# Output projection as seven block products, late modulation sums on ScalarE with adding transfers

## The chip, the cores and the metric

The kernel runs on one core of a Trainium2 chip. The metric is the device time of one execution in microseconds. The engines are TensorE (PE; its weight loads are listed as PEld), VectorE (DVE), ScalarE (ACT), GpSimd (POOL) and SyncE (SP). SP and POOL issue the transfers; transfers that add to what is in memory (`accum_op`) are issued by POOL.

## The reference, cut

One residual block on x (512 tokens x 1024) with a conditioning vector c. Everything is float32.

```python
mod = silu(c) @ w_ada + b_ada      # shift1, scale1, gate1, shift2, scale2, gate2
h = rms_norm(x, g_pre_mix) * (1 + scale1) + shift1
z = h @ w_in                       # [GLU | q latent | kv latent | rotary key | gates]
u = ua * sigmoid(ub)
u = silu(layer_norm(causal_depthwise_conv(u, 31 taps)))
y_a = u @ w_conv_out
y_b = mla_attention(...) @ w_attn_out          # 8 heads
y = (sigmoid(g_a) * y_a + sigmoid(g_b) * y_b) @ w_out
x = x + gate1 * rms_norm(y, g_post_mix)
h = rms_norm(x, g_pre_mlp) * (1 + scale2) + shift2
x = x + gate2 * rms_norm(relu(h @ w_mlp_in)**2 @ w_mlp_out, g_post_mlp)
```

## The kernel before, in words

**Number format.** A float32 product is made of three fp32r products (`mm3`, L476): each operand is split into a high part (a ScalarE cast) and a low part (a VectorE difference). `split` (L481) does that for an operand, `W` (L494) for a loaded weight, and `wunit` (L514) loads and splits one. So each 1024-wide weight costs one cast and one difference.

**Order of the work.** The code does not issue instructions at once. Every call is recorded as an `Op` (`Planner.record`, L262), and all of them are issued by one line, L410, which is why every row of the profile names L410. `Planner.plan` (L325) gives each operation a due time, worked back from TensorE's sequence with a price for each operation (`cost`, L234), and then runs a list schedule in which each engine takes the ready operation of the earliest due time, less its `hurry` (L346); TensorE takes the ready one of the lowest rank, which is its order in the program less a `boost`. `plan.after` adds a dependence on an earlier operation. The result is one fixed order for each engine; engines and transfer queues work in that order. Buffers come from two arenas in on-chip memory, `f_arena` (22400 words a partition) and `r_arena` (28000, for the split parts), and from eight PSUM banks. `Arena.alloc` (L90) places buffers with the lifetimes of the pass before, up to 14 passes are made, and the plan that is shortest by the planner's own prices is issued.

**Stages.** First the modulation for the first norm and the input projection; then the latents and the attention, head by head (`proj`, `scores`, `pv`). VectorE fills its time with the 31-tap convolution: `pump(n)` (L836) puts n of its 248 taps at a place in the program. Then come the attention's output product, the two gate products, the layer norm, and the conformer's product with `co_evac` (L1324), which forms the mixed tensor (gate a times y_a plus gate b times y_b) and splits it.

**Late modulation.** Parts 2, 3 and 4 of the modulation (gate1, shift2, scale2) are needed only after the output projection. `ada_units` (L1167) loads w_ada in units of 256 rows x 1024 columns (1 MB), twelve units in all, and sums them on VectorE, eight operations of 1024 columns for each part. `take` (L1184) puts units at places in the program, here from the gate products on. `late_mod` (L1359) adds the partitions up with TensorE and forms the gate row `G1` and the columns `mod[:, 2]` and `mod[:, 3]`.

**Output projection.** 192 fp32r products of 512 columns: token tile by token tile (four of 128), two halves of 512 output columns, eight blocks of 128 input rows, three products each. All tiles' first halves are made first (`ys[t, 0]`), then the late modulation, then the second halves, tile by tile. After two tiles (`for tp in range(2)`, L1411) these are normed (squares on ScalarE, the power on POOL, the scaling and the residual sum on VectorE), normed again for the MLP, written out, transposed on TensorE and scaled and split into `h2`, the MLP's input. The first hidden products of the MLP work on 256 columns (the first two token tiles), so that they can run while the other two tiles are finished.

**MLP.** The second MLP product is already made by `strassen` (L1486) in four chunks: seven products of 256 x 512 blocks with sums and differences of blocks for eight products. Each of its products needs up to one left operand (a 1024-wide sum and a split) and one right operand (two 1024-wide weights, their difference and splits). Partial results are added to memory (`y_spill`) with adding transfers of 256 KB on POOL.

Of the kernel before, what the change touches and what calls it, by code (L numbers as in the profile page):

```python
# [51 lines left out]
ADAS = (1, 1, 0, 4)  # L52
KGRP = ((2,), (3,), (4,), (5,), (6,), (7,))
# [361 lines left out]
def tile_hybrid_block(  # L415
# [30 lines left out]
    hD = [tc.dram_tile([P, KD * T], F32, name=f"h_spill{i}") for i in range(2)]  # L446
    yD = [tc.dram_tile([P, D], F32, name=f"y_spill{t}") for t in range(NT)]
# [16 lines left out]
    def emit(past, replay):  # L464
# [682 lines left out]
        rope_half(0)  # L1147
        proj(0)
        proj(1)
        scores(0)  # L1150
        for h in range(H):
            if h + 2 < H:
                proj(h + 2)
            if h == 2:
                rope_half(1)
            if h + 1 < H:
                scores(h + 1)
            pv(h)
            pump(PUMPS[2])
        for q in qkv:  # L1160
            ra.free(*q)
        ra.free(K1, K2)


# [151 lines left out]
        take(late, ADAS[3])  # L1316
# [5 lines left out]
        mT = []  # L1322

        def co_evac(ct, b):  # L1324
            m = fa.alloc(T)
            dve.scalar_tensor_tensor(fa.v(m), fa.v(ta[ct]), 1.0, pb.v(b), op0=ALU.add, op1=ALU.mult)
            dve.tensor_tensor(fa.v(m), fa.v(m), fa.v(yb[ct]), ALU.add)
            hl = pair(T)
            split(fa.v(m), *hl)
            mT.append(hl)  # L1330
            fa.free(m, ta[ct], yb[ct])
            take(late, ADAS[0])

# [25 lines left out]
        def late_mod():  # L1359
            G1 = gate_row(2, g_post_mix, 0.5)  # L1360
# [18 lines left out]
        xr = []  # L1379
        for t in range(NT):  # L1380
            b = fa.alloc(D)
            sp.dma_start(out=fa.v(b), in_=x[t * P:(t + 1) * P, :])
            xr.append(b)
        h2, h2f, h2s_ = [], [], {}

        def k4(a):
            return a.rearrange("p (k t) -> p k t", k=4)

        def yl(t, k):
            return ra.v(mT[k][0])[:, t * P:(t + 1) * P], ra.v(mT[k][1])[:, t * P:(t + 1) * P]  # L1390

        ys = {(t, 0): pb.alloc() for t in range(NT)}
        for k0 in range(0, KD, 2):
            w = wunit(w_out, k0, 0, 2, 512)
            for k in range(2):
                for t in range(NT):
                    mm3(pb.v(ys[t, 0]), yl(t, k0 + k), w(k, 0, 512), k0 + k == 0, k0 + k == KD - 1)
            w.free()
        take(late)
        G1 = late_mod()  # L1400
        ys.update({(t, 1): pb.alloc() for t in range(NT)})
        wo = [wunit(w_out, k0, 512, 2, 512) for k0 in range(0, KD, 2)]
        NCH = 4
        HPC = FF // P // NCH

        def hid_weights(n0, n, i0=0):

            return {(i, kh): wunit(w_mlp_in, 4 * kh, (n0 + i) * P, 4, 256) for i in range(i0, n, 2) for kh in range(2)}

        ws0 = {(0, 0): wunit(w_mlp_in, 0, 0, 4, 256)}  # L1410
        for tp in range(2):  # L1411
            xn = []
            for t in (2 * tp, 2 * tp + 1):
                for k in range(KD):
                    mm3(pb.v(ys[t, 1]), yl(t, k), wo[k // 2](k % 2, 0, 512), k == 0, k == KD - 1)
                    if t == NT - 1 and k % 2 == 1:
                        wo[k // 2].free()
# [383 lines left out]
```

## Time and profile before

| | |
|---|---|
| median of 3 runs | 813.99 us (813.33 to 814.12) |
| the profiled execution | 812.54 us, span 810.4 us |
| granted TensorE clock | 0.998 |
| TensorE busy | 790.7 us |
| VectorE busy | 738.0 us |
| ScalarE busy | 472.0 us |
| POOL busy | 62.8 us |
| bytes moved | 131.00 MB |

Busy time counts the union of an engine's instructions; matmuls are pipelined, so the mean duration in a row is longer than the time that each takes of the engine. A row of a group gives line, engine, operation, tile written and tiles read, shapes and count, then busy us and mean ns of one, then the idle time of the engine before them and who ended it. All tiles in the two arenas carry the arena's name. "CUSTOM_DVE_ANT_0" is the VectorE instruction that also sums (`tensor_tensor_reduce`).

### The profile page before, as it was taken

What the parts mean: (1) busy time and instruction counts of PE and PEld (TensorE: products, weight loads), DVE (VectorE), ACT (ScalarE), POOL (GpSimd) and SP (SyncE); (2) the same over time, 40 slices, a digit from 0 to 9 for tenths busy, and PEclk for the clock granted to TensorE, in tenths of its full rate; (3) what the DMA queues carried; (4) which work ended last, traced back from release to release, by engine and by line L of the source; (5) the groups of instructions that cost most, each with busy time, mean ns of one, the idle gap of its engine ahead of it and who ended that gap; (6) DMA issues with size and microseconds to landing.
All of it is one profiled execution on the core that took longest, in us unless ns stands there. A gap on an engine that the chain in (4) does not pass through costs nothing. (4 is left out here: it accounts for less than half of the span.)

```text
span 810.4 us, 11974 instructions
## 1 busy us (share of the span) xinstructions
PE 790.7 (98%) x4450; PEld 687.7 (85%) x4450; DVE 738.0 (91%) x1045; ACT 472.0 (58%) x784; POOL 62.8 (8%) x121
## 2 busy tenths in 40 slices
PE   6999999999999999999999999999999999999996
PEld 3778988889897888888888879988998899889985
DVE  3898999999999999999997579899689999996997
ACT  5455463365885247229243378677667756777851
POOL 2001010000000000000000021001002200320023
PEclk9999999999999999999999999999999999999999
DMA  9989433112352160064998044159317991895076
GB/s 295 313 247 341 144 116 110 53 53 66 105 170 78 53 202 5 1 222 162 344 391 281 7 159 148 53 149 266 132 53 157 243 343 37 171 288 178 28 164 134
DMA packets 99981, 131.00 MB, mean 162 GB/s; under 512 B 8433, under 2 KB 67154, under 8 KB 99922
## 3 DMA queue, kind: packets, MB, share of 16 engines
q1 hardware_dynamic: 93586, 118.69, 45.1%
q0 software_dynamic: 6336, 11.54, 8.9%
q8 instruction: 35, 0.57, 0.3%
q14 instruction: 24, 0.20, 0.1%
HBM read 109.23 MB, written 20.97 MB: 161 GB/s over the span
## 5 line engine op out<-in xcount | busy, mean ns | idle before, releaser
L410 PE MATMUL psum<-r_arena 128*128 128x512 f32 (+3 forms) x4108 | 751.1, 344 | 4.0 <-DVE f_arena L410 1.6
L410 PEld LDWEIGHTS psum<-r_arena 128*128 128x128 f32 x4108 | 647.6, 189 | 91.7 <-ACT r_arena L410 2.7
L410 ACT CAST r_arena<-f_arena 128x1024 fp32r<-128x1024 f32 (+5 forms) x249 | 235.2, 966 | 137.3 <-PE psum L410 86.4
L410 DVE TENSOR_TENSOR r_arena<-f_arena,r_arena 128x1024 fp32r<-128x1024 f32 (+5 forms) x259 | 276.1, 1093 | 28.0 <-PE psum L410 15.1
L410 DVE SCALAR_TENSOR_TENSOR f_arena<-f_arena,cw 128x512 f32<-128x512 f32 x240 | 164.2, 737 | 0.0
L410 DVE TENSOR_TENSOR f_arena<-f_arena 128x1024 f32<-128x1024 f32 (+3 forms) x108 | 113.6, 1071 | 4.7 <-ACT f_arena L410 2.4
L410 ACT ACTIVATE f_arena<-f_arena 128x512 f32<-128x512 f32 (+4 forms) x121 | 71.3, 607 | 42.9 <-DVE f_arena L410 42.0
L410 ACT COPY f_arena<-psum 128x512 f32<-128x512 f32 (+4 forms) x103 | 55.3, 547 | 41.5 <-PE psum L410 36.9
L410 DVE SCALAR_TENSOR_TENSOR f_arena<-f_arena,cT 128x256 f32<-128x256 f32 (+1 forms) x70 | 55.9, 800 | 1.2
L410 POOL DMA_DIRECT2D y_spill<-f_arena x40 | 34.8, 879 | 263.6 <-ACT f_arena L410 254.8
L410 ACT ACTIVATE f_arena<-psum 128x512 f32<-128x512 f32 x43 | 25.2, 593 | 45.4 <-PE psum L410 44.3
L410 PE MATMUL psum<-ident,f_arena 128*128 128x128 f32 (+1 forms) x234 | 34.8, 288 | 7.9 <-DVE f_arena L410 7.9
L410 PEld LDWEIGHTS psum<-ident,f_arena 128*128 128x128 f32 (+1 forms) x234 | 28.3, 147 | 14.0 <-DVE f_arena L410 9.3
L410 ACT CAST r_arena<-psum 128x512 fp32r<-128x512 f32 (+2 forms) x57 | 30.0, 562 | 12.7 <-PE psum L410 12.4
L410 DVE TENSOR_TENSOR r_arena<-psum,r_arena 128x512 fp32r<-128x512 f32 (+2 forms) x57 | 35.6, 653 | 0.9 <-ACT r_arena L410 0.6
L410 DVE TENSOR_TENSOR f_arena<-psum,f_arena 128x512 f32<-128x512 f32 (+1 forms) x34 | 22.3, 666 | 7.7 <-PE psum L410 7.6
L410 POOL TENSOR_TENSOR stats<-stats,nhalf 128x1 f32<-128x1 f32 (+1 forms) x17 | 15.5, 915 | 172.3 <-ACT stats L410 156.3
L410 POOL TENSOR_TENSOR lns<-lns,nhalf 128x4 f32<-128x4 f32 x1 | 1.4, 1400 | 249.5 <-DVE lns L410 249.5
L410 ACT ACTIVATE r_arena<-f_arena 128x256 fp32r<-128x256 f32 (+3 forms) x17 | 10.9, 642 | 14.4 <-DVE f_arena L410 11.3
L410 ACT ACTIVATE r_arena<-f_arena,mod 128x512 fp32r<-128x512 f32 x8 | 6.5, 816 | 21.6 <-DVE mod L410 21.6
L410 DVE TENSOR_SCALAR f_arena<-f_arena,stats 128x1024 f32<-128x1024 f32 x8 | 6.0, 753 | 13.6 <-POOL stats L410 13.6
L410 DVE CUSTOM_DVE_ANT_0 f_arena<-psum,mask 128x128 f32<-128x128 f32 (+3 forms) x32 | 14.6, 481 | 0.0
(98 smaller groups left out, 211.1 us busy)
## 6 DMA issues: line engine op xcount, KB each, us to landing
f_arena<-in_w_ada_dram SPq DMA_DIRECT2D x16, 1024.0 KB
f_arena<-in_w_mlp_in_dram SPq DMA_DIRECT2D x32, 512.0 KB
f_arena<-in_w_mlp_out_dram SPq DMA_DIRECT2D x32, 512.0 KB
f_arena<-in_w_in_dram SPq DMA_DIRECT2D x24, 512.0 KB
y_spill<-f_arena POOLq DMA_DIRECT2D x40, 256.0 KB, 6.2
f_arena<-in_w_ada_dram SPq DMA_DIRECT2D x32, 256.0 KB
f_arena<-in_x_dram SPq DMA_DIRECT2D x8, 512.0 KB
h_spill<-r_arena SPq DMA_DIRECT2D x16, 256.0 KB
```

What stands on the lines that cost most here:

```text
L410: getattr(self.real[o.eng], o.fn)(*o.a, **o.k)
```

## The change

It has three parts. First, the output projection is made by `strassen`, which gets a function for its left operand and a function `used` that is called when the first half of it is no longer needed. The mixed tensor is kept as two float32 buffers `mF` (not split). `mix_block` receives each block of results: the first contribution to a block is copied from PSUM, the second is added to it, and a tile that is complete is normed, and a pair of complete tiles goes through `to_hidden` (the second half of the old loop). `late_mod` is called once the first block is complete, after the second of seven products. Second, the late sums are made in the attention: each unit is loaded, multiplied by its column of silu(c) on ScalarE in place, and written (the first of a part, SP) or added (the other seven, POOL) to a buffer `aD` in memory; `late_mod` loads the three sums. Third, in `strassen` itself the difference s3, the split of block 22 and the difference t3 are recorded ahead of the fifth product.

```diff
+ADAQ = (1, 1, 1, 2, 2, 2, 2, 1)
+ADAH = 5e4
...
+    aD = {q: tc.dram_tile([P, D], F32, name=f"a_spill{q}") for q in (2, 3, 4)}
...
+        def ada_sums(parts):
+            for part in parts:
+                for u in range(4):
+                    plan.hurry, plan.after = ADAH, len(plan.ops) - 1
+                    b = fa.alloc(2 * D)
+                    v = fa.v(b, "p (j n) -> p j n", j=2)
+                    sp.dma_start(out=v, in_=w_ada[u * 256:(u + 1) * 256, part * D:(part + 1) * D].rearrange("(j p) n -> p j n", p=P))
+                    plan.after = None
+                    for jj in range(2):
+                        j = u * 2 + jj
+                        act.mul(v[:, jj], v[:, jj], cT[:, j:j + 1])
+                        if j == 0:
+                            sp.dma_start(out=aD[part], in_=v[:, jj])
+                        else:
+                            pool.dma_start(out=aD[part], in_=v[:, jj], accum_op=ALU.add)
+                    fa.free(b)
+                    plan.hurry = 0.0
+                    yield
...
+        late = ada_sums((2, 3, 4))
         for h in range(H):
...
             pv(h)
             pump(PUMPS[2])
+            take(late, ADAQ[h])
...
-        late = ada_units((2, 3, 4))
-            if ct % 2:
-                take(late, ADAS[2])
-        take(late, ADAS[3])
...
         def co_evac(ct, b):
-            m = fa.alloc(T)
-            dve.scalar_tensor_tensor(fa.v(m), fa.v(ta[ct]), 1.0, pb.v(b), op0=ALU.add, op1=ALU.mult)
-            dve.tensor_tensor(fa.v(m), fa.v(m), fa.v(yb[ct]), ALU.add)
-            hl = pair(T)
-            split(fa.v(m), *hl)
-            mT.append(hl)
-            take(late, ADAS[0])
+            if ct % 4 == 0:
+                mF.append(fa.alloc(4 * T))
+            m = k4(fa.v(mF[-1]))[:, ct % 4]
+            dve.scalar_tensor_tensor(m, fa.v(ta[ct]), 1.0, pb.v(b), op0=ALU.add, op1=ALU.mult)
+            dve.tensor_tensor(m, m, fa.v(yb[ct]), ALU.add)
...
         def late_mod():
+            for part in (2, 3, 4):
+                ada_acc[part] = load(D, aD[part])
...
-        def strassen(hv, block, banked, parts=1):
+        def strassen(A, block, banked, used, parts=1):
...
             dve.tensor_tensor(a3(s4), A(0, 1), a3(s2), ALU.subtract)
-            product(a_form(a3(s4)), b_form(b22), bb, False)
+            s3 = fa.alloc(1024)
+            dve.tensor_tensor(a3(s3), A(0, 0), A(1, 0), ALU.subtract)
+            used()
+            w22 = b_form(b22)
+            t3 = b12
+            b_sub(t3, b22, b12)
+            fa.free(*b22)
+            product(a_form(a3(s4)), w22, bb, False)
...
+        def mix_block(mi, nh, bs):
+            n = seen[mi, nh] = seen.get((mi, nh), 0) + 1
+            done = n == (1 if (mi, nh) == (1, 0) else 2)
+            for tt in range(2):
+                t = 2 * mi + tt
+                y, ps, s = fa.v(ysb[t])[:, sl], pb.v(bs[tt]), nrm[t]
+                if not done:
+                    act.copy(y, ps)
+                    continue
+                if (mi, nh) == (1, 0):
+                    y = ps
+                else:
+                    dve.tensor_tensor(y, ps, y, ALU.add)
...
+                        dve.tensor_tensor_reduce(ra.v(j), y, y, 0.25 / D, s[:, 1:2], ALU.mult, ALU.add, s[:, 2:3])
+                    pool.tensor_tensor(s[:, 2:3], s[:, 2:3], nhalf[:, :1], ALU.pow)
...
+                xr = load(D, x[t * P:(t + 1) * P, :])
...
+            if xn:
+                to_hidden(mi, xn)
+            if (mi, nh, n) == (0, 0, 2):
+                G1[0] = late_mod()
...
+        strassen(lambda i, j: k4(fa.v(mF[j]))[:, :, 256 * i:256 * i + 256], blocks_of(w_out, 0), mix_block,
+                 lambda: fa.free(mF[0]))
```

The rest of `mix_block` and `to_hidden` are the steps of the old loop over `tp`, moved.

More of the change, by code (lines that the diff above doesn't have):

```diff
@@ L1145, in pv @@
                     ra.free(vh, vl)
[L1147 to L1162, printed above, removed]
         ada_acc = {}
@@ L1187, in take @@
                     return
-        late = ada_units((2, 3, 4))
+        late = ada_sums((2, 3, 4))
+        rope_half(0)
+        proj(0)
+        proj(1)
+        scores(0)
+        for h in range(H):
+            if h + 2 < H:
+                proj(h + 2)
+            if h == 2:
+                rope_half(1)
+            if h + 1 < H:
+                scores(h + 1)
+            pv(h)
+            pump(PUMPS[2])
+            take(late, ADAQ[h])
+        for q in qkv:
+            ra.free(*q)
+        ra.free(K1, K2)
         def feat_gemm(wsrc, c0, rhs, evac, pumped=0, groups=(2, 2, 2, 2)):
@@ L1467, in emit @@
-        fa.free(G1)
-        def h2s(k, a, n):
-            return tuple(ra.v(b)[:, a:a + n] for b in h2[k])
-        ysb = {}
-        G2, fin = None, []
-        late = ada_units((5,))
+        h2, h2f, h2s_ = [], [], {}
         def blocks_of(wsrc, k0):
@@ L1556, in strassen @@
             pb.free(*bb)
-            s3 = fa.alloc(1024)
-            dve.tensor_tensor(a3(s3), A(0, 0), A(1, 0), ALU.subtract)
-            t3 = b12
-            b_sub(t3, b22, b12)
             product(a_form(a3(s3)), b_form(t3), ba, False)
-            fa.free(s3, *t3, *b22)
+            fa.free(s3, *t3)
             banked(1, 1, ba)
@@ new lines, in to_hidden @@
+        def to_hidden(tp, xn):
+            if tp == 1:
+                fa.free(mF[1])
+                ws0[0, 1] = wunit(w_mlp_in, 4, 0, 4, 256)
+                ws0.update(hid_weights(0, 4, 2))
+            if tp == 0:
+                ws0[0, 0] = wunit(w_mlp_in, 0, 0, 4, 256)
+                h2[:] = [pair(T) for _ in range(KD)]
+                h2f[:] = [fa.alloc(4 * T) for _ in range(2)]
+            hsl = slice(tp * 256, (tp + 1) * 256)
+            for k2 in range(KD // 2):
+                b = pb.alloc()
+                for q in range(2):
+                    for t in range(2):
+                        k = 2 * k2 + q
+                        pe.transpose(pb.v(b)[:, (2 * q + t) * P:(2 * q + t + 1) * P], fa.v(xn[t])[:, k * P:(k + 1) * P], ident)
+                for q in range(2):
+                    k = 2 * k2 + q
+                    ps, v = pb.v(b)[:, q * 256:(q + 1) * 256], k4(fa.v(h2f[k // 4]))[:, k % 4, hsl]
+                    hb, lb = (ra.v(z)[:, hsl] for z in h2[k])
+                    if k == 0:
+                        act.activation(hb, ps, AF.Identity, scale=mod[:, 3, k:k + 1], bias=mod[:, 2, k:k + 1])
+                        dve.tensor_scalar(v, ps, mod[:, 3, k:k + 1], mod[:, 2, k:k + 1], ALU.mult, ALU.add)
+                    else:
+                        act.activation(v, ps, AF.Identity, scale=mod[:, 3, k:k + 1], bias=mod[:, 2, k:k + 1])
+                        act.copy(hb, v)
+                    dve.tensor_tensor(lb, v, rf(h2[k][0])[:, hsl], ALU.subtract)
+                pb.free(b)
+            fa.free(*xn)
@@ L1569, in h2_sums, with h2s @@
+        strassen(lambda i, j: k4(fa.v(mF[j]))[:, :, 256 * i:256 * i + 256], blocks_of(w_out, 0), mix_block,
+                 lambda: fa.free(mF[0]))
+        fa.free(G1[0])
+        def h2s(k, a, n):
+            return tuple(ra.v(b)[:, a:a + n] for b in h2[k])
+        ysb = {}
+        G2, fin = None, []
+        late = ada_units((5,))
         def h2_sums():
```

128 lines of the change are left out of this document (42 added, 86 removed).

## The prediction

> **What bounds the kernel now.** I read the page first (busy time, the slices), then the windows by stage, then the groups by shape and the order of time of TensorE around the output projection, and last the waits of TensorE.
>
> ```profile
> span 810.4 us, 11974 instructions
> PE 790.7 (98%) x4450; PEld 687.7 (85%) x4450; DVE 738.0 (91%) x1045; ACT 472.0 (58%) x784; POOL 62.8 (8%) x121
> PE   6999999999999999999999999999999999999996
> DVE  3898999999999999999997579899689999996997
> ```
>
> TensorE (PE) works through the whole span but for its two ends; VectorE (DVE) is nearly as full, with one visible gap (the 7, 5 and 7). So the kernel is bound by TensorE, with VectorE close behind. Columns of the windows are length, then busy us of PE, PEld, DVE, ACT and POOL with their instructions, granted clock, DMA share and GB/s:
>
> ```profile
> 150.00:235.00 85.00, 84.19 (x536) 75.90 (x535) 84.07 (x190) 56.03 (x129) 0.00 (x0) 1.00 0.26 80
> 345.00:430.60 85.60, 85.60 (x391) 70.68 (x390) 84.08 (x120) 42.37 (x66) 1.40 (x1) 1.00 0.81 286
> 430.60:452.00 21.40, 21.40 (x96) 17.74 (x95) 9.13 (x10) 5.92 (x11) 0.00 (x0) 1.00 0.56 181
> 452.00:481.50 29.50, 28.16 (x144) 23.06 (x142) 22.12 (x32) 15.27 (x41) 5.23 (x7) 1.00 0.20 72
> ```
>
> The first is most of the attention, the second the gate and conformer products, the last two the output projection. TensorE's waits between 20 and 790 us add up to only 4.1 us:
>
> ```profile
> PE psum L410 <- DVE f_arena L410: 1.6, 3, 1.1
> PE psum L410 <- ACT f_arena L410: 1.4, 2, 1.1
> PE psum L410 <- ACT r_arena L410: 0.8, 2, 0.6
> PE psum L410 <- DVE r_arena L410: 0.3, 1, 0.3
> ```
>
> A change gains here only by taking products off TensorE, and it loses wherever VectorE or a chain then comes late.
>
> **Part 1: products removed.** The output projection is 4 token tiles x 2 halves x 8 blocks x 3 = 192 products of 512 columns; seven block products of 2 x 4 x 3 make 168. The price of one is from a stretch without other work (362.3 to 440):
>
> ```profile
> L410 PE MATMUL psum<-r_arena 128*128 128x512 f32 x343 | 78.0, 389 | 0.0
> ```
>
> 78.0/343 = 0.2274 us (the mean of 389 ns holds pipelining), so 24 fewer are **-5.46 us**. Shapes are unchanged, and the transposes and the late modulation's products stay.
>
> **Part 2: VectorE in this stage.** What goes: the 24 late sums, and 8 weight splits and 8 half-size splits of the mixed tensor, replaced by others.
>
> ```profile
> L410 DVE SCALAR_TENSOR_TENSOR f_arena<-f_arena,cT 128x1024 f32<-128x1024 f32 x21 | 26.8, 1279 | 0.2
> L410 DVE TENSOR_SCALAR f_arena<-f_arena,cT 128x1024 f32<-128x1024 f32 x3 | 2.2, 748 | 0.2 <-DMA f_arena<-in_w_ada_dram 0.2
> L410 DVE TENSOR_TENSOR r_arena<-f_arena,r_arena 128x1024 fp32r<-128x1024 f32 x16 | 19.3, 1215 | 0.4 <-ACT r_arena L410 0.2
> L410 DVE TENSOR_TENSOR f_arena<-f_arena 128x1024 f32<-128x1024 f32 x9 | 11.0, 1218 | 0.1
> L410 DVE TENSOR_TENSOR f_arena<-psum,f_arena 128x512 f32<-128x512 f32 x2 | 1.3, 686 | 7.3 <-PE psum L410 7.3
> L410 DVE CUSTOM_DVE_ANT_0 r_arena<-f_arena,stats 128x512 fp32r<-128x512 f32 x3 | 2.2, 743 | 0.0
> ```
>
> Removed: 26.8 + 2.2 = 29.0 us of sums, 8 x 1.215 = 9.7 of weight splits, 8 x 0.68 = 5.4 of the others (a 512-wide two-input operation costs as the 0.686 above). Added at 1.217 for a 1024-wide operation: 14 weight splits 17.0, 7 splits of the left operand 8.5, 4 + 8 sums and differences 14.6; 6 adds from PSUM 4.1; 2 squares with sum 1.5. The balance is 45.7 against 44.1: VectorE gets +1.6 us in a stage that TensorE leaves 5.5 us earlier. Over 345 to 481.5 it had 136.5 - 84.1 - 9.1 - 22.1 = 21.2 us idle, so about 14 remain.
>
> The idle time does not lie where the work does. The window from 430.6 to 452.0 holds 96 products, the first half of the output projection, so the conformer's last product ends near 430.6; its first evacuation of the last pair can start 12 x 0.2274 = 2.7 us earlier. From there to the first hidden product VectorE must do: 17.0 + 8.5 + 14.6 + 4.1 + 1.5 from above, 2.7 of last evacuations, the late modulation 6.8, the norms of two tiles 6.9 and half of the hidden input 3.9, two first weights of the MLP 2.4; in all 68.4 us. The last four come from rows of 452 to 500:
>
> ```profile
> L410 DVE SCALAR_TENSOR_TENSOR f_arena<-psum,stats,f_arena 128x512 f32<-128x512 f32 x8 | 5.6, 746 | 1.8 <-POOL stats L410 1.8
> L410 DVE TENSOR_SCALAR f_arena<-f_arena,stats 128x1024 f32<-128x1024 f32 x4 | 3.0, 754 | 5.2 <-POOL stats L410 5.2
> L410 DVE TENSOR_REDUCE f_arena<-psum 128x4 f32<-128x512 f32 x4 | 2.6, 681 | 0.0
> L410 DVE TENSOR_TENSOR r_arena<-f_arena,r_arena 128x256 fp32r<-128x256 f32 x16 | 6.0, 416 | 0.0
> ```
>
> (a tile's norm is 2 x 0.75 + 1.22 + 0.75; the late modulation 1.2 + 1.4 + 1.2 + 2.7 and 0.3 of small ones; the hidden input's half 8 x 0.416 and one of 0.5.) What can run ahead, into the 29 us that the sums leave before 430.6, is what depends on weights and on the first half of the mixed tensor, as far as the arenas hold it: three weight forms (7.3), eight differences of weights (9.7; most in place), the first left form and one difference (2.4): 19.4. The other 49.0 us from 427.9 would be done at 476.9.
>
> **Part 3: when TensorE gets on.** In order of time (start, us):
>
> ```profile
> 467.78 0.66 PE L410 MATMUL psum<-ident,f_arena 128*128 128x128 f32 x4
> 468.19 0.47 PE L410 MATMUL psum<-r_arena 128*128 128x512 f32 x1
> 469.15 0.71 PE L410 MATMUL psum<-r_arena 128*128 128x512 f32 x2
> 469.84 4.14 PE L410 MATMUL psum<-r_arena 128*128 128x512 f32 x17
> 473.82 1.07 PE L410 MATMUL psum<-ident,f_arena 128*128 128x128 f32 x8
> 474.65 5.80 PE L410 MATMUL psum<-r_arena 128*128 128x512 f32 x29
> 481.55 0.62 PE L410 MATMUL psum<-r_arena 128*128 128x256 f32 x3 [1.10 <-ACT f_arena L410]
> ```
>
> The products from 468.19 on are 49: one of token tile 1 and the 48 of tiles 2 and 3. So tile 1 ends near 468.4; its norm, transposes and evacuations let the first hidden product start at 481.55, 13.15 us later, while TensorE's cover lasts to 480.45. After the change tiles 0 and 1 end with the fifth block product, and the sixth and seventh are the cover: 2 x 5.46, as before. TensorE would be through at 480.45 - 5.46 = 475.0. The chain behind the fifth product loses three ScalarE steps,
>
> ```profile
> L410 ACT ACTIVATE f_arena<-psum 128x512 f32<-128x512 f32 x8 | 4.7, 592 | 12.7 <-PE psum L410 12.7
> L410 ACT ACTIVATION_READ_ACCUMULATOR f_arena<-psum 128x1 f32 x8 | 1.6, 194 | 0.0
> L410 ACT ACTIVATE stats<-stats 128x1 f32<-128x1 f32 x4 | 1.2, 294 | 0.1
> ```
>
> and gets an add (0.69) and a square with sum (0.74) on VectorE: +0.4. And the splits of products six and seven, six operations of 1.217, compete with it: from none (all ahead) to 7.3; I take one, since the chain left VectorE idle (the 5.2 us of waits for POOL above), so **+1.6**, bounds +0.4 and +7.7. The hidden products would start at 481.55 - 5.46 + 1.6 = 477.7, which the 476.9 of the count allows.
>
> Tile 2 now ends 12 x 0.2274 = 2.7 us before tile 3, where it was 5.5: a norm of 3.5 us of VectorE moves behind the seam, whose cover (96 products of 256 columns) stays. Bounds 0 and +2.7; a shorter square for tile 3 speaks for the low end: **+0.6**.
>
> **Part 4: the late sums in the attention.** 24 ScalarE products of 1024 columns, nearest row:
>
> ```profile
> L410 ACT ACTIVATE f_arena<-f_arena 128x1024 f32<-128x1024 f32 x4 | 4.2, 1061 | 7.4 <-DVE f_arena L410 7.4
> L410 DVE SCALAR_TENSOR_TENSOR f_arena<-f_arena,cw x80: 729/735/746, 74.9 to 150.8; 128x512 f32<-128x512 f32 x80
> L410 DVE SCALAR_TENSOR_TENSOR f_arena<-f_arena,cw x123: 721/736/748, 74.9 to 232.2; 128x512 f32<-128x512 f32 x123
> ```
>
> They cost 25.4 us. Their loads hang on convolution taps 77 to 126 of 248 (the last operations recorded before them), which run at about 145 to 232. ScalarE is idle 29.0 of the 85 us there, so it becomes 96% busy. Queued behind a product that waits for its load are the softmax and the casts that TensorE needs; the planner puts the products behind these by due time, and each can hold one up by at most 1.06. TensorE's waits for ScalarE are the 1.4 and 0.8 above over nearly the whole kernel; I take **+0.3** (bounds 0 and +2.2, twice those waits). On SP the three first writes wait for ScalarE with the attention's weights behind them: nothing, since DMA is 0.26 busy and the loads have lead; uncovered, a 1.06 each. The 12 loads of 1 MB leave 345 to 402, where DMA is 0.81 busy; three loads of 512 KB come instead: nothing, as TensorE is busy 85.60 of 85.60 us there with them in place. POOL: below. The reordered steps of the MLP's own products are not priced: the same helper runs there without a wait,
>
> ```profile
> 600.00:640.00 40.00, 40.00 (x198) 33.79 (x197) 38.96 (x36) 30.65 (x39) 10.04 (x12) 1.00 0.67 144
> ```
>
> and bounds are +-1.1, TensorE's longest wait.
>
> **Sum**: -5.46 + 1.6 + 0.6 + 0.3 = -3.0 us. The profiled execution took 812.54 us (1.45 below the median 813.99), so 809.5 by its own time and **811.0** by the median.
>
> **Rivals.** *A, the full saving.* The seam costs no more than now, as in the 600 to 640 window, where VectorE is at 97% and TensorE at 100%: 813.99 - 5.5 = 808.5. Against it: there the hidden stage lies before each set of products, here 68 us of VectorE's work meet 47.
>
> *B, VectorE becomes the bound.* The hidden stage starts later than now as soon as less than 68.4 - (481.55 - 427.9) = 14.8 us have run ahead. If the arenas let only two weight forms and four differences through (9.7), it starts at 427.9 + 58.7 = 486.6, 5.05 later than now, with the 0.9 of the other terms 813.99 + 5.95 = 819.9: slower. For it: four weight blocks, the mixed tensor, the conformer's weights and the held results fill f_arena's 22400 words nearly. Against it: the gap of 430 to 452, with 9.13 of 21.4 us used.
>
> *C, POOL's chain of adding transfers.* Every addition waits for the one before to land, in order on one queue.
>
> ```profile
> L410 POOL DMA_DIRECT2D y_spill<-f_arena x40: 856/862/1117, 536.2 to 787.0; - x40
> DMA to landing us min/median/max: 3.6/6.2/9.9
> q0 software_dynamic: 6336, 11.54, 8.9%
> ```
>
> Those carry 256 KB, and move at 0.089 x 810.4 / 44 = 1.64 us each; 512 KB should land in 7.8 us (bounds 5.2 and 11.5). 24 steps from 145 on end near 332 (270 to 420), far behind the 232 of the loads but before the gate is needed at 452: no cost by itself. But the planner's code reckons 1.1 + 2.7 + 1.1 = 4.9 us a step, so buffers would be handed to others up to 24 x 2.9 = 70 us before they are free; a ScalarE or VectorE instruction that meets one late landing holds its queue for 7.8: 811.0 + 7.8 = 818.8. It decides once a successor is planned within that lag.
>
> [...]
>
> **How the numbers follow.** The forecast 0.48, A 0.20, B 0.20, C 0.12. About 0.2% (1.6 us) is what a measurement of this kernel can tell from no change. Faster: 0.42 of the forecast (its terms above +3.8 leave too little) and all of A, 0.62. Same: 0.05 of the forecast, 0.07 of B's beginning, 0.01 of C: 0.13. Slower: the rest, 0.25. The low end is the full saving with 1.5 of the present waits gone: 807.0; the high end takes in the beginning of B and most small forms of C: 818.0. The likeliest case alone is 808 to 813.
>
> **What would show it.** 168 products in the stage; no late sums on VectorE after 345; ScalarE over 90% in 150 to 235 with TensorE's waits there under 2 us; POOL's additions until about 330; the first hidden product (256 columns) near 477.7. Wrong if that product starts after 480, if TensorE waits over 3 us in the attention, or if an engine waits for an adding transfer.

## The result and the profile after

| | before | after |
|---|---|---|
| median | 813.97 us (of this comparison) | 835.83 us (833.25 to 839.27, 4 runs) |
| profiled execution, its span | 812.54 us, 810.4 us | 833.25 us, 831.5 us |
| granted TensorE clock | 0.998 | 0.990 |
| ScalarE busy | 472.0 us | 505.4 us |
| POOL busy | 62.8 us | 85.9 us |

The ratio is 1.0273, with a 95% interval of 1.0231 to 1.0315: slower by 2.7%, where 0.4% faster was forecast. From the page (busy time; the slices of TensorE and of its clock; then packets, MB and share of the DMA engines of POOL's queue):

```profile
span 831.5 us, 12033 instructions
PE 792.5 (95%) x4426; PEld 687.0 (83%) x4426; DVE 741.6 (89%) x1048; ACT 505.4 (61%) x813; POOL 85.9 (10%) x142
PE   6999999979999997999999989999999989999996
PEclk9999999999999998999999999999999999999999
q0 software_dynamic: 9360, 22.55, 16.7%
```

TensorE has its 24 products fewer (4426 for 4450), yet its slices show dips at 166 us and at 312 us (the 9th and the 16th), which the kernel before didn't have (smaller ones follow at 478 and 665 us), and the clock shows one at 312. Both lie in the attention, where no product was removed or added. The windows of the stage, the last two also for the kernel before:

```profile
150.00:235.00 85.00, 78.92 (x495) 71.02 (x494) 75.78 (x167) 62.78 (x124) 8.61 (x10) 0.96 0.75 194
235.00:300.00 65.00, 63.46 (x315) 52.59 (x314) 62.88 (x119) 43.08 (x81) 5.19 (x6) 1.00 0.93 256
300.00:345.00 45.00, 39.13 (x172) 31.79 (x172) 38.56 (x50) 24.73 (x50) 3.46 (x4) 0.92 0.70 191
```

```profile
235.00:300.00 65.00, 64.65 (x308) 53.58 (x307) 64.89 (x108) 33.35 (x60) 0.00 (x0) 1.00 0.39 112
300.00:345.00 45.00, 45.00 (x211) 36.92 (x210) 45.00 (x66) 21.25 (x48) 0.00 (x0) 1.00 0.08 28
```

From 150 to 235 us TensorE made 495 products; it had made 536. The DMA share was 0.26, 0.39 and 0.08 in the three stretches and is 0.75, 0.93 and 0.70. ScalarE is no bound by its amount of work: 62.78 of 85 us. TensorE's waits in the whole run:

```profile
PE psum L412 <- DVE f_arena L412: 11.0, 5, 7.6
PE psum L412 <- ACT f_arena L412: 8.5, 4, 5.9
PE psum L412 <- ACT r_arena L412: 8.2, 5, 5.8
PE psum L412 <- DVE r_arena L412: 3.2, 3, 1.5
```

With 0.8 of small ones that is 31.7 us. The whole run before had 12.5 us, most of it one wait at the start that the changed kernel has too:

```profile
PE psum L410 <- DVE f_arena L410: 9.6, 5, 7.4
```

So there are 19.2 us more. In order of time (the bracket is the idle time before the row and what ended it):

```profile
186.34 8.21 PE L412 MATMUL psum<-r_arena 128*128 128x512 f32 x37 [5.84 <-ACT r_arena L412]
320.58 1.11 PE L412 MATMUL psum<-ident,f_arena 128*128 128x128 f32 x4 [5.87 <-ACT f_arena L412]
487.84 3.97 PE L412 MATMUL psum<-r_arena 128*128 128x512 f32 x16 [1.91 <-DVE f_arena L412]
497.29 1.22 PE L412 MATMUL psum<-r_arena 128*128 128x256 f32 x8 [1.46 <-DVE r_arena L412]
```

Two waits for ScalarE in the attention make 11.7 us. ScalarE's rows just ahead of the first:

```profile
183.03 2.19 ACT L412 ACTIVATE f_arena<-f_arena,cT 128x1024 f32<-128x1024 f32 x2 [5.79 <-DMA f_arena<-in_w_ada_dram]
185.13 0.60 ACT L412 ACTIVATE f_arena<-f_arena 128x384 f32<-128x384 f32 x1
185.72 1.32 ACT L412 CAST r_arena<-psum 128x512 fp32r<-128x512 f32 x3
```

Two late-sum products stood at the head of ScalarE's queue and waited 5.79 us for their 1 MB load. The softmax step (185.13) and the casts that TensorE needs (185.72) stood behind them. The load itself, and what SP's queue waited for just before it (164.6 to 178.0 us):

```profile
177.65 1.04 SPq L412 DMA_DIRECT2D f_arena<-in_w_ada_dram  x2
SPq L412 <- DMA a_spill<-f_arena: 13.0, 1, 13.0
```

The load left at 177.65, and its product began at 183.03, 5.4 us later. So this transfer was hardly slower than the 4.9 us of the plan (below); it was late because SP had stood 13.0 us for an addition. Ahead of the second wait:

```profile
311.33 1.08 ACT L412 COPY f_arena<-psum 128x512 f32<-128x512 f32 x2 [4.27 <-DMA a_spill<-f_arena]
319.93 0.60 ACT L412 ACTIVATE f_arena<-psum 128x512 f32<-128x512 f32 x1 [3.36 <-DMA a_spill<-f_arena]
```

These two have nothing to do with the late sums. Their output buffer was a late sum's before, handed on by the plan before the adding transfer that reads it had landed (the releaser is the addition). Who waited between 120 and 340 us, first all engines, then SP's queue:

```profile
POOL a_spill L412 <- DMA a_spill<-f_arena: 68.3, 11, 8.4
...
ACT f_arena L412 <- DMA f_arena<-in_w_ada_dram: 22.7, 7, 10.1
...
ACT f_arena L412 <- DMA a_spill<-f_arena: 7.6, 2, 4.3
...
PE psum L412 <- ACT r_arena L412: 7.2, 2, 5.8
...
PE psum L412 <- ACT f_arena L412: 6.4, 2, 5.9
```

```profile
SPq L412 <- DMA a_spill<-f_arena: 76.4, 11, 16.7
```

So the chain is: POOL's additions wait for each other (68.3 us); SP, which must load into buffers that these additions still read, stands for 76.4 us, with the attention's other loads behind; the loads go out late; ScalarE waits 22.7 us for them, in order, and TensorE 7.2 + 6.4 = 13.6 us for ScalarE. The landing times, of the additions and of the loads:

```profile
L412 POOL DMA_DIRECT2D a_spill<-f_arena x21: 853/865/1089, 140.5 to 326.2; - x21
DMA to landing us min/median/max: 5.1/6.0/10.4
```

```profile
L412 SPq DMA_DIRECT2D f_arena<-in_w_ada_dram x12: 367/376/2677, 130.2 to 290.4; - x12
DMA to landing us min/median/max: 7.1/10.7/11.1
```

By the planner's formula, which the kernel's code holds, each of them takes 4.9 us (1.1 + 2.73 + 1.1, the factor 2 for POOL making 512 KB as dear as the load of 1 MB). The middle addition is thus 1.1 us later than planned. The second row is of three loads only: for the other nine the trace tells no landing. Their products began 5.3 to 11.6 us after the issue, which bounds it.

And each of these two waits is followed by half clock (columns as in the windows above; the granted clock is the third number from the end):

```profile
186.30:190.00 3.70, 3.66 (x9) 3.08 (x10) 3.70 (x8) 2.80 (x9) 0.00 (x0) 0.50 0.68 124
190.00:194.00 4.00, 4.00 (x27) 3.67 (x27) 2.56 (x6) 3.88 (x7) 0.86 (x1) 0.99 0.68 102
320.50:324.00 3.50, 3.42 (x10) 2.90 (x11) 3.44 (x6) 1.71 (x5) 0.47 (x1) 0.50 1.11 324
324.00:328.00 4.00, 4.00 (x17) 3.30 (x16) 4.00 (x7) 2.16 (x8) 0.86 (x1) 0.68 0.45 65
```

In the first stretch seven products of 512 columns and two of 384 took 3.66 us, some 0.43 us for each 512 columns, where the prediction's price at full clock is 0.2274. The clock that was missing is 3.70 x 0.50 + 3.50 x 0.50 + 4.00 x 0.32 = 4.9 us. The account of the span (+21.1 us): -5.46 of products, +19.2 of waits, +4.9 of clock; the other +2.5 I can't place.

Comparing the start of the same product in both traces (counted from the start up to the output projection, from the end behind it) gives the loss by place, in times of the kernel before: +1.0 us at 126 us, +8.3 at 180, +10.5 at 287, +19.3 at 330, +20.1 at 462, +17.9 behind the output projection, +21.4 at the end. The output projection gave 2.2 us back; the attention had taken 18.3.

### The profile page after: what moved, and what is told of

It is laid out like the page before. It is cut to its first block, busy times and chain, and to the rows that moved or that the text cites. A ratio compares the mean times of both kernels' runs of the same rounds, so it can differ in the third digit from the quotient of the medians.

```text
span 831.5 us, 12033 instructions
## 1 busy us (share of the span) xinstructions
PE 792.5 (95%) x4426; PEld 687.0 (83%) x4426; DVE 741.6 (89%) x1048; ACT 505.4 (61%) x813; POOL 85.9 (10%) x142
## 4 chain that ended last, share of the span: by engine, by line
PE 76%; DVE 12%; DMA 6%; ACT 3%; issue 2%; POOL 1%; DVEq 0%; POOLq 0%; SPq 0%; ACTq 0%
PE psum L412 76%; DVE f_arena L412 6%; DVE r_arena L412 6%; DMA a_spill<-f_arena 3%; DMA f_arena<-in_w_ada_dram 2%; ACT f_arena L412 2%; ACT r_arena L412 1%; POOL stats L412 1%; DMA f_arena<-in_x_dram 0%; DMA f_arena<-y_spill 0%; DVE mod L412 0%; DVEq L1826 0%; ACT stats L412 0%; POOLq L1826 0%; SPq L412 0%
## 5 line engine op out<-in xcount | busy, mean ns | idle before, releaser
L412 ACT CAST r_arena<-f_arena 128x1024 fp32r<-128x1024 f32 (+5 forms) x254 | 244.2, 982 | 127.2 <-PE psum L412 95.8
L412 DVE TENSOR_TENSOR r_arena<-f_arena,r_arena 128x1024 fp32r<-128x1024 f32 (+5 forms) x264 | 285.7, 1113 | 39.6 <-PE psum L412 25.0
L412 DVE TENSOR_TENSOR f_arena<-f_arena 128x1024 f32<-128x1024 f32 (+3 forms) x120 | 128.3, 1086 | 5.9 <-ACT f_arena L412 2.4
L412 PE MATMUL psum<-ident,f_arena 128*128 128x128 f32 x234 | 36.2, 295 | 14.1 <-DVE f_arena L412 7.6
L412 PEld LDWEIGHTS psum<-ident,f_arena 128*128 128x128 f32 x234 | 30.0, 152 | 20.1 <-DVE f_arena L412 8.1
L412 ACT ACTIVATE f_arena<-f_arena,cT 128x1024 f32<-128x1024 f32 x24 | 26.6, 1147 | 22.7 <-DMA f_arena<-in_w_ada_dram 22.7
L412 POOL DMA_DIRECT2D a_spill<-f_arena x21 | 18.3, 874 | 195.5 <-DMA a_spill<-f_arena 68.3
L412 DVE SCALAR_TENSOR_TENSOR f_arena<-f_arena,cT 128x256 f32<-128x256 f32 (+1 forms) x49 | 29.2, 596 | 0.9
L412 ACT ACTIVATE r_arena<-f_arena 128x512 fp32r<-128x512 f32 (+3 forms) x21 | 13.4, 639 | 13.8 <-DVE f_arena L412 11.3
L412 DVE SCALAR_TENSOR_TENSOR f_arena<-f_arena 128x512 f32<-128x512 f32 (+1 forms) x18 | 13.3, 744 | 3.0 <-ACT f_arena L412 3.0
```

The costliest lines, as they stand in the source:

```text
L412: getattr(self.real[o.eng], o.fn)(*o.a, **o.k)
```

## The experiments

The theory: transfers leave or land later than the plan reckons, and engines that work in a fixed order stand behind them. Its rivals: the amount of work put on ScalarE; VectorE in the output stage; the new order in `strassen`; plain re-planning, since any edit gives another plan. Kernels with prices added have four lines more, so their rows name L416. Each ratio is to the kernel before in the same comparison, with its 95% interval.

### Which part loses

**Block products alone**, the late sums on VectorE at their old places:

```diff
-        late = ada_sums((2, 3, 4))
+        late = ada_units((2, 3, 4))
...
-            take(late, ADAQ[h])
```

(`take` again behind the gate products and in `co_evac`, and `take(late)` in `late_mod`.)

> The seven block products with the late sums left on VectorE, at their old places behind the gate products. Theory Q (the queue: in the attention ScalarE's products wait in order for loads that come late, because the adding transfers hold the buffers): the attention has no such product here, so the time is 808 to 815, and what the block products give (3.6 us at the first hidden product in the changed kernel) and give back behind it (3.7) is what is left. Theory V (VectorE is the bound of the output projection, rival B): VectorE has 29 us of sums more in that stage than in the changed kernel, so the time is 825 or more.

**Sums alone**, with the old output projection:

```diff
             pump(PUMPS[2])
+            take(late, ADAQ[h])
...
-        late = ada_units((2, 3, 4))
+        late = ada_sums((2, 3, 4))
```

> The old output projection with the late sums on ScalarE and adding transfers during the attention. Theory Q: 832 to 840, TensorE's waits for ScalarE in 150 to 345 add up to 10 us or more. Theory V: within 3 us of the kernel before.

Block products alone: 817.29 us, 1.0054 [1.0041, 1.0067], between the two ranges expected. Sums alone: 831.80 us, 1.0242 [1.0217, 1.0266], just short of theory Q's range and far from theory V's. The sums alone bring the two waits of the changed kernel, in its own places:

```profile
185.60 7.96 PE L412 MATMUL psum<-r_arena 128*128 128x512 f32 x37 [5.59 <-ACT r_arena L412]
321.11 1.11 PE L412 MATMUL psum<-ident,f_arena 128*128 128x128 f32 x4 [5.83 <-ACT f_arena L412]
```

and SP's queue again waits 82.7 us for the additions. Block products alone lose too, elsewhere. Its row of TensorE, and the window of the output projection:

```profile
473.81 1.22 PE L412 MATMUL psum<-r_arena 128*128 128x512 f32 x2 [5.72 <-ACT r_arena L412]
```

```profile
430.60:481.50 50.90, 44.50 (x201) 36.63 (x200) 50.04 (x60) 29.81 (x46) 2.68 (x4) 0.93 0.40 134
```

VectorE is busy 50.04 of 50.90 us, TensorE waits 5.72 us and is granted 0.93 of its clock in the window; by equal products this stage went from +1.7 to +6.2. The wait itself ends with a cast of ScalarE, but it is VectorE that has no time left. That is what the prediction's rival B feared, here in a kernel that leaves the 29 us of sums on VectorE.

### Amount of work, or lateness

**No chain**: the same 24 ScalarE products and the same loads, but each result is plainly written to a place of its own. What this leaves out: nothing adds the 24 results up, and `late_mod` uses the first of each part.

```diff
-    aD = {q: tc.dram_tile([P, D], F32, name=f"a_spill{q}") for q in (2, 3, 4)}
+    aD = {(q, j): tc.dram_tile([P, D], F32, name=f"a_spill{q}_{j}") for q in (2, 3, 4) for j in range(8)}
...
-                            pool.dma_start(out=aD[part], in_=v[:, jj], accum_op=ALU.add)
+                            pool.dma_start(out=aD[part, j], in_=v[:, jj])
```

> The changed kernel with each of the 24 products written to a place of its own in memory by a plain transfer from the same queues; the sums are left out (only the first product of each part is read back). Theory Q with the chain as its cause (an addition waits for the one before, so buffers come free late and loads start late): 808 to 818. Theory Q with the loads as its cause (1 MB lands in 10.7 us where 4.9 were planned): 825 or more, with ScalarE still waiting 15 us or more for these loads.

**Priced**: the changed kernel, all its work kept; the planner alone is told that the 12 loads land 6 us later and the 24 writes and additions 3 us later.

```diff
+LOAD_FAR, ADD_FAR = 6000.0, 3000.0
...
+        o.far = self.far if fn == "dma_start" else 0.0
+        o.post += o.far
...
-                        o.t1 = dma_free + 1100.0
+                        o.t1 = dma_free + 1100.0 + o.far
```

> The changed kernel, but the planner reckons 6 us more until a load of the late sums has landed and 3 us more for each of their first writes and additions; nothing else differs. Theory Q: orders and buffers are then planned for what the transfers take, TensorE's waits in 150 to 345 fall below 4 us, and the time is 808 to 816. Theory W (27 us of work more on ScalarE are what hurts, not waits): still 828 or more.

No chain: 814.33 us, 1.0012 [1.0001, 1.0022]. Priced: 815.52 us, 1.0042 [1.0024, 1.0060]. The window of the first, and TensorE's waits between 100 and 345 us in the second:

```profile
150.00:235.00 85.00, 84.25 (x534) 75.64 (x533) 83.97 (x191) 70.56 (x144) 8.51 (x16) 1.00 0.78 268
```

```profile
PE psum L416 <- ACT f_arena L416: 0.6, 2, 0.4
PE psum L416 <- DVE r_arena L416: 0.2, 1, 0.2
```

ScalarE does more here (70.56 us) than in the changed kernel, at the same DMA share (0.78), and TensorE makes 534 products where that made 495. So neither the amount of work on ScalarE nor a DMA share of that size is the cause. And with the additions kept and only the prices mended, the 13.6 us of waits for ScalarE in the attention shrink to 0.8 of all waits. Both times lie in the ranges of theory Q. A price changes the whole plan, so one priced kernel could be luck; but all four other kernels below with both prices and at least eight of the twelve units in the attention lie at -0.25 to +0.67%, and those without prices at +1.7 to +2.7%, one more, a bad plan at large, at +7.2%. So that the loss comes from lateness against the plan is shown. The 6 and 3 us themselves are not measured transfer times: the load above left late and took 5.4 us at most.

**Each price alone**, the other left at zero (`LOAD_FAR, ADD_FAR = 6000.0, 0.0` and `0.0, 3000.0`):

> The changed kernel, with only the loads of the late sums reckoned 6 us longer by the planner (additions as in the changed kernel). If the loads' price is what went wrong: 813 to 819. If it is the additions' price: 828 or more, since buffers are still handed out too early.

> The changed kernel, with only the first writes and additions reckoned 3 us longer by the planner. If the additions' price is what went wrong, because it sets when buffers come free and so when loads start: 813 to 819. If it is the loads' price: 828 or more, ScalarE still waiting 15 us or more for loads.

Loads alone: 823.52 us, 1.0113 [1.0097, 1.0129]. Additions alone: 825.02 us, 1.0136 [1.0113, 1.0160]. SP's wait for additions in the one and in the other (120 to 340 us):

```profile
SPq L416 <- DMA a_spill<-f_arena: 59.6, 11, 13.8
```

```profile
SPq L416 <- DMA a_spill<-f_arena: 0.5, 1, 0.5
```

With the loads priced, ScalarE no longer waits for them, but SP is still held, and now the attention's own weights come late (ScalarE waits 13.7 us for the output weights, 12.2 for the input weights). With the additions priced, SP is free, but ScalarE waits 8.3 us for late-sum loads and 21.8 for input weights, and TensorE once more for 7.7:

```profile
314.57 1.12 PE L416 MATMUL psum<-ident,f_arena 128*128 128x128 f32 x4 [7.74 <-ACT f_arena L416]
```

Each price alone takes away about half of the loss, both together nearly all. Both expectations asked for one culprit (813 to 819, or 828 and more), and both times lie between.

**A wider margin instead of prices**: a place in an arena is taken without charge only if its last holder is planned to be gone 3.0 us before, not 1.5.

```diff
-    SLACK = 1500.0
+    SLACK = 3000.0
```

> The changed kernel with the same one constant (3.0 us for 1.5) and nothing else: loads and additions have their old, too short prices. Theory T (the loads land some 6 us and the additions some 3 us later than planned, and both must be in the due times): 1.5 us of margin covers neither, TensorE still waits over 10 us between 120 and 345 us, and the median is 825 to 840. Rival H (what hurts is only that places are handed over before additions have landed, which a margin cures as well as a price): under 5 us of waits there, 814 to 820.

827.28 us, 1.0171 [1.0147, 1.0195]. The wait at 320 us is gone (it was the handed-on buffer), the first one stays, behind SP's 76.0 us:

```profile
189.25 6.75 PE L412 MATMUL psum<-r_arena 128*128 128x384 f32 x30 [4.67 <-ACT r_arena L412]
```

The attention costs 7.5 us of waits here, below the 10 expected, and the time is where the theory put it, 8.6 us below the changed kernel. A margin at the hand-over cures the hand-over; the rest of the loss stays.

### Without the late sums

Both of these leave the late sums out: `late_mod` loads three row blocks of w_ada in their place. The first keeps the block products, the second is the kernel before.

```diff
-            take(late, ADAQ[h])
...
-                ada_acc[part] = load(D, aD[part])
+                ada_acc[part] = load(D, w_ada[0:P, part * D:(part + 1) * D])
```

> The block products with the late sums left out on every engine (one row block of each part is loaded in their place): what the block products do by themselves, beside the run with the old products and no sums. Theory S (the first hidden product comes 4 us earlier, but the norms of tiles 2 and 3 then lie close together and behind VectorE's splits, so all of it is lost again at the second seam): the two differ by less than 1.5 us. Theory of the forecast (0.6 us lost there): this one is 3 to 4 us faster.

> The kernel before with the late sums left out on every engine (one row block of each part is loaded in their place). TensorE hardly waited in the gate and conformer stages, so 812 to 814: the sums cost nothing where they stood, and taking them off VectorE brings nothing by itself.

Block products without sums: 812.01 us, 0.9975 [0.9966, 0.9984]. The old projection without sums: 821.10 us, 1.0078 [1.0061, 1.0096]: a kernel with less work is slower. So neither expectation held: the second run missed 812 to 814, and the two differ by 9.1 us. By equal products the first went from +1.8 to -2.0 us in the output projection, 3.8 us gained, and lost 3.6 in the MLP. The trace of the second (an execution of 817.37 us, the fastest of six) is level with the kernel before up to the output projection (-0.2 us), +3.1 behind it, and then has in the MLP, whose code was not touched,

```profile
739.66 29.06 PE L410 MATMUL psum<-r_arena 128*128 128x256 f32 x240 [2.57 <-ACT f_arena L410]
```

That looks like another plan's misfit, and is a warning: a difference of some us between two kernels here can come from the plan alone.

### Order and plan

**Priced, with the MLP's products recorded in the old order**, and **the new order alone, in the kernel before**:

```diff
-            w22 = b_form(b22)
-            t3 = b12
-            b_sub(t3, b22, b12)
-            product(a_form(a3(s4)), w22, bb, False)
+            product(a_form(a3(s4)), b_form(b22), bb, False)
...
+            t3 = b12
+            b_sub(t3, b22, b12)
             product(a_form(a3(s3)), b_form(t3), ba, False)
```

(the first as shown, in the MLP only; the second the reverse of it.)

> As e3 (both prices), with the new recording order inside the block products kept for the output projection and undone for the four products of the MLP. Theory O (that order costs 3 us in the MLP, where e3 and the kernel without additions lost that much): 3 us faster than e3, 811 to 813. Theory P (the MLP's waits are only another plan's): within 2 us of e3 in either direction, and the MLP's waits are elsewhere but not gone.

> The kernel before with the new recording order of the block products alone, in the MLP. Theory O: 816 to 818, the loss behind 520 us. Theory P: 812.5 to 815.5.

819.42 us, 1.0067 [1.0052, 1.0081], and 814.88 us, 1.0012 [1.0003, 1.0020]. The new order costs the kernel before some 1 us, as theory P has it. Taking it out of the priced kernel met neither range: the loss behind the output projection went (6.0 us with it, 0.0 without), but the new plan got a wait of 3.49 us at 311.6, where ScalarE stood 3.72 us for an input weight. Between the output projection and the end the products lose 3.5 us in the changed kernel, 3.1 without a chain, 6.0 priced, but only 0.3 with sums alone and nothing (-1.1) with block products alone, which has the new order too. The block products without sums, in the new order, lose 3.6 there. Of the kernels with the old order that follow, two gain 0.5 and one (all sums behind the attention) loses 6.1. So the order alone neither makes the loss nor rules it out; what does is not settled. Each figure is of one execution, that of the priced kernel 2.9 us above its median, that without sums 1.8.

**The kernel before with another plan**, the same work: 4 passes of the planner for 14.

```diff
-PASSES = 14
+PASSES = 4
```

> The kernel before with 4 placement passes for 14: the same work, another plan. It shows how far a new plan alone moves the time. Theory P (plans of one work differ by several us, which is what hides the saving of the block products in the runs so far): 1 to 6 us from the kernel before, in either direction. If plans are alike: within 1 us.

812.81 us, 0.9988 [0.9977, 1.0000]: 0.8 us by the medians, so theory P missed, and these two plans are alike.

### Where the sums could go

All of these keep the prices and the MLP's old order, unless said. **One unit a head**, the other four behind the attention's output product; **all twelve behind the attention**:

```diff
-ADAQ = (1, 1, 1, 2, 2, 2, 2, 1)
+ADAQ = (1, 1, 1, 1, 1, 1, 1, 1)
...
             yb.append(y)
+            if ct % 2:
+                take(late, 1)
```

(the other: `ADAQ = (0,) * 8`, one unit with each evacuation there and four behind the next product.)

> As e9, with one unit of the late sums for each head and the other four behind the attention, so that the adding chain is asked for 16 steps where it was asked for 24. Theory Q: the prices already keep loads and additions off the path, so this gives at most 1 us more than e9 (810 to 813). If the crowd of transfers itself costs, 2 us or more.

> As e9, with all twelve units behind the attention, in the attention's output product and the first gate product, where DMA was 0.08 to 0.39 busy and ScalarE half idle in the kernel before. Theory Q: no softmax is queued behind a late load, 809 to 813. If the chain of 24 steps of 6 to 8 us then ends too late for the gate row (needed near 440): 816 or more, with TensorE waiting near 440.

One a head: 814.91 us, 1.0011 [1.0000, 1.0022], 4.5 us below the priced kernel with the old order, where theory Q allowed 1; but that kernel has the wait at 311.6, so this doesn't show that the crowd of transfers costs. All behind: 827.82 us, 1.0178 [1.0155, 1.0201], where theory Q had 809 to 813. TensorE waits 1.62, 0.80, 2.23 and 0.87 us for ScalarE and VectorE between 380 and 413, not near 440 as the rival had it, and 2.19, 2.56 and 3.40 us at 356, 482 and 672. The attention was the better place.

Three relatives of "one a head": the new order in the MLP as well; `SLACK = 3000.0` as well; and no prices (with the new order).

> As e11, but with the new recording order in the MLP's products too. Theory O: 2 to 3 us slower than e11, behind 520 us. Theory P: within 3 us of e11 in either direction, with the difference spread over stages.

> As e11, with 3.0 us for 1.5 between the planned end of one owner of a buffer and the next. If handing buffers over too early is what still costs e11 its 3 us: 808 to 812. Theory P: 811 to 818.

> The changed kernel with one unit for each head and four behind the attention, without new prices. If the rate asked of the chain (two units for each of four heads) is the cause: 812 to 818. If it is the planner's prices, at any rate: 824 or more, with TensorE waiting over 5 us in 150 to 345.

With the new order 814.93 us, 1.0021 [1.0008, 1.0034], within 1 us of the old, as theory P has it. With the wider margin **812.08 us, 0.9975 [0.9962, 0.9988]**, the fastest kernel here that leaves nothing out. Without prices 872.55 us, 1.0724 [1.0703, 1.0745], by far the slowest. Of the last, a row of TensorE:

```profile
97.61 0.66 PE L412 MATMUL psum<-r_arena 128*128 128x352 f32 x1 [7.43 <-DVE f_arena L412]
```

It waits for VectorE before the first late product is made, and again in every stage (20.4 us for splits by VectorE in all). Asking for the sums at a lower rate does not help by itself; but this kernel's loss is a bad plan at large, and I can't lay it to the missing prices alone.

**The margin alone, in the kernel before**, tells what the fastest version owes to it:

> The kernel before with one constant changed: the arenas take a place as free of charge only if its last holder was planned to be gone 3.0 us earlier instead of 1.5. It settles what the fastest version so far (812.08, 0.25% below the kernel before) owes to this constant and what to the change. Theory T (lateness of transfers in the attention is the cause, and the wider margin only helps where buffers are held by transfers that land late): TensorE waits only some 3.5 us in the whole kernel before, so the median stays within 2 us of it, 812 to 816. Rival S (the margin alone makes any plan better): 810 to 811.5, as much below the kernel before as the fastest version lies below its own twin without the margin (2.8 us).

816.28 us, 1.0041 [1.0019, 1.0063], with runs from 813.21 to 823.13 us: no gain, rather a loss, so rival S is out, and theory T's range is just missed. So the 0.25% of the fastest version isn't the margin's by itself. But it is one plan out of several tried, its siblings lie at +0.1 and +0.2%, and its profiled execution (813.34 us, the second slowest of its twelve) isn't faster than the one before, so that no trace shows where the 1.5 to 2 us come from. I take it as measured and unexplained.

## Why the prediction was wrong, point by point

**Part 1** held: 24 products fewer, and the output projection pays them back. In the version without a chain, by equal products, it went from +1.6 to -1.8 us: -3.4, where -5.46 + 1.6 + 0.6 = -3.26 was forecast.

**Part 2** held as a balance: VectorE's work in the whole run grew by 741.6 - 738.0 = 3.6 us, where +1.6 was forecast for the stage. With the sums gone VectorE carries the stage; with them kept there (block products alone) it doesn't, as rival B feared for another reason, the room in the arenas.

**Part 3** was right in its sum, with a misread row. The row of 29 products at 474.65 is named for its first form; grouped by form, 478.0 to 481.5 us of the kernel before hold

```profile
L410 PE MATMUL psum<-r_arena 128*128 128x256 f32 x10 | 1.4, 282 | 0.0
```

So ten hidden products already ran before the wait at 481.55; the first began at 479.10. Then only 39 of the 49 products are of the output projection, and tile 2 begins with nine more, ahead of the rows shown:

```profile
465.69 2.20 PE L410 MATMUL psum<-r_arena 128*128 128x512 f32 x9
```

So tile 1 ends near 465.7 and the cover near 479.1, 2.7 and 1.4 us earlier than the prediction reads them, and the time between tile 1 and the first hidden product hardly changes (13.4 us for 13.15). In the version without a chain the same product begins at 476.98; the first row has TensorE's longest wait there, the second the hidden product among the products of 475.05 to 477.5:

```profile
469.11 3.92 PE L412 MATMUL psum<-r_arena 128*128 128x512 f32 x16 [1.69 <-DVE f_arena L412]
L412 PE MATMUL psum<-r_arena 128*128 128x256 f32 x1 | 0.3, 276 | 0.0
```

That is -2.1, and -3.7 less its own +1.6: the first seam cost 1.7 (forecast 1.6), the second +0.3 (forecast 0.6). Worked from the right row, the forecast time of this product is 479.10 - 5.46 + 1.6 = 475.2, and 476.98 - 1.6 = 475.4 was measured; that 476.98 lies near the forecast 477.7 is luck. In the changed kernel the product begins at 495.55.

**Part 4 is the step that failed**: "+0.3 (bounds 0 and +2.2)". The sums alone cost 831.80 - 813.37 = 18.4 us. Three sentences of it were wrong.
- It named the queue behind a product that waits for its load, and then priced each hold by the product's own 1.06 us. The hold is the lateness of the load, 5.79 us in the case above, because SP stood 13.0 us before it could send that load.
- It put the wait of SP at "nothing, since DMA is 0.26 busy". That share was of the kernel before. The change itself brings the 12 MB of loads and the additions, and the share is 0.70 to 0.93. Nor was the share the point: SP waited 76.4 us for buffers, and without a chain a share of 0.78 brings no such loss.
- It found no cost in POOL's chain, since the chain ends in time. The last addition leaves at 326 us and lands near 331.5 (forecast 332), but the chain holds buffers, SP waits for buffers, and SP has the attention's weights behind.

Another term of it, the reordered steps of the MLP at nothing with bounds of 1.1 us, measured +1.2 us in the kernel before, just outside.

**Rival C** had the mechanism and was sized as one hold of 7.8 us, at a chance of 0.12. There were two of nearly 6, smaller ones, and the half clock after them. Its landing time of 7.8 us (bounds 5.2 and 11.5) was too long for the middle addition, 6.0 us. The 21 additions landed in 5.1 to 10.4 us.

**The signs named** did their work: TensorE waited 13.6 us in the attention (the limit was 3), engines waited for adding transfers, and the product awaited before 480 came at 495.55. ScalarE was not at 90% but at 74%, as it stood waiting.

**What is left of the gain** once the cause is gone: the versions with mended prices and at least eight of the twelve units in the attention lie at -0.25 to +0.67%. The forecast was -0.37%: the fastest of them comes near it (-0.25%, interval to -0.38%), and none comes near rival A's full saving (-0.67%). The gain of 3.4 us in the output projection is there in the version without a chain. By the traces 1 to 2 us go in the first 75 us and up to 6 in the MLP; but a trace is one execution, and executions of the kernel before lay between 812.0 and 816.0 us in one comparison, so that 1 to 2 us can't be laid to the plan.

## What to carry to other kernels

A transfer moved into a stage has to be priced with what it waits for and with what waits for it there, not by the DMA share that the profile shows without it. Where engines work in a fixed order, a late transfer can delay every queue that stands behind it, as here, where between 120 and 340 us SP stood for 76.4 us, ScalarE for 22.7 and TensorE for 13.6: list the queues that need its buffer, too. Before judging a re-planned kernel, time the old one under another plan; two such plans moved it by -0.1 and +0.4%.

## What the runs showed of the hardware

**The clock after a wait.** By the clock's record of the changed kernel, TensorE's waits of 5.84 and 5.87 us each brought 6.8 us at half clock (183.2 to 190.1 us and 319.8 to 326.6), part of it in the wait itself; the one that ended at 320.58 cost 3.0 us more than itself. For other kernels, what the mean clock of a window lacks of 1.00, times its length, is the clock that was missing, to some tenths of a us: some 3.6 us with a wait of 7.74 us (additions alone priced, 0.92 from 300 to 345 us) and with one of 5.72 (block products alone, 0.93 from 430.6 to 481.5), 1.6 with one of 3.40 (priced, 0.98 from 600 to 680), and 1.8 with waits of 1.26 and 2.33 us, 5 us apart (loads alone priced, 0.96 from 300 to 345). A wait of 1.91 us that ended at 480.74 in that same kernel went with some 1.6 (0.99 from 430 to 482, 0.97 from 482 to 520); one of 1.91 us that ended at 487.84 in the changed kernel brought none (1.00 from 484 to 510). With one of 2.83 us (one a head) the whole run was granted 0.998, as the kernel before was. So the length of a wait alone doesn't tell what it costs in clock.

**The price of an addition.** POOL's queue held all 16 engines for 0.089 x 810.4 = 72.1 us before and 0.167 x 831.5 = 138.9 us after: 66.7 us for 21 additions of 512 KB, 3.2 us each. With plain writes of the same size (the version without a chain, span 813.3 us) its row is

```profile
q0 software_dynamic: 9360, 22.55, 12.7%
```

that is 103.3 us, or 1.5 us each, if the queue's other transfers took the same time in all three runs. By this estimate an addition held the engines twice as long as a plain write; its landing, as the trace has it, took longer still: 6.0 us in the middle, up to 10.4 in the crowd.
